# More expert groups ahead of layer 0's dense stage, gate multiplies on ScalarE, and split weights in the latent DeltaNet

## The chip, the cores and the metric

The kernel runs on one core of a Trainium2 chip. The core has TensorE (PE) for matmuls, VectorE (DVE), ScalarE (ACT) and GpSimd (POOL) for elementwise work, SyncE (SP), which issues most of the DMAs, and 16 DMA engines; each engine works its own instructions in order and waits for others by semaphores. The metric is the device time of one execution in microseconds (us). Three executions of the kernel before took 4279.19, 4285.04 and 4299.03 us; the median is 4285.04.

## The reference

The reference computes one block (a mixer of three branches and a convolutional feed-forward), and then a second block with two layers, each a mixer and a PEER layer, over 256 latent tokens and 256 context tokens of width 1024. The mixer of layer 0 is a gated DeltaNet, that of layer 1 attention. What the change touches is the DeltaNet and PEER:

```python
# PEER: 8 heads, 128 x 128 experts, 16 chosen per head
qry = (xb @ w_query).reshape(P, PEER_HEADS, 2, PEER_HALF)
s = jnp.einsum('phcd,hckd->phck', qry, sub_keys)
top_s, top_i = lax.top_k(s, PEER_TOPK)
...                       # 256 candidates of two halves, top 16 again
gate = jax.nn.softmax(best_s, axis=-1)
act = jax.nn.gelu(jnp.einsum('pd,phkd->phk', xb, u_tab[idx]))
coef = gate * act
return jnp.einsum('phk,phkd->pd', coef, v_tab[idx])
# DeltaNet
proj = h @ w_in           # 1024 -> 6208: q, k, v, z, gates
...                       # causal chunks of 64 tokens, 16 heads, both directions
return (rmsnorm_2(o, norm_g) * silu(z)).reshape(B, T, 2048) @ w_out
```

## The kernel before

The program runs, in order: conditioning vectors, the DeltaNet over the context tokens (51 to 580 us of the profiled execution), the first block (580 to 1550), the DeltaNet over the latent tokens (1550 to 2215), the latent PEER layer 0 (2215 to 3235), attention (to about 3440) and the latent PEER layer 1 with the final norm. The context tokens' PEER layer is worked differently from the latent one: its chosen experts are gathered from DRAM by index (POOL, L1908), multiplied and summed on DVE (dots L1931 `sg`, sums L1937 `spy`). This sparse work is a generator that other stages draw from (`bg`, with rates `bg_l`, `bg_dense` and the like), so its instructions stand between theirs on DVE and POOL.

A latent PEER layer (`peer_lat`) treats all experts densely, in 128 groups of 128. It has these stages:

- Routing (`route`): scores on PE (L1782), top-k on DVE. Since PE has little to do there, `ahead` gives it the u products of the first 20 groups, with plain f32 weights (L2018), into tiles `ge`. Behind the last top-k, indices `gi` and gates `gate` are transposed on PE (L1966) into `gT`.
- Building G (`build_G`): for each token a 128 x 128 matrix of gates, as a product of two one-hot matrices. For four tokens, DVE compares an iota with the second index (`gB`, L1979) and, token by token, with the first index and multiplies by the gate (`gA`, L1986); PE multiplies (L1989), ACT evicts (`Gs`, L1990), SP stores it in DRAM (`d_G`).
- Dense stage: for each group g, `dense_c` multiplies the activations `ge` with G and splits the result in two (`ch`, `cl`, L2030 to L2035); `dense_v` loads and splits the v weights (`vh` on ACT L221, `vl` mostly on POOL L222, every second one on DVE from group 108) and multiplies (L2054 to L2056, accumulators `acc`); `dense_u` makes the u product of group g + 20 with split weights (`uh` on ACT, `ul` on DVE; `mm3`, L226 to L228). From group 108 on there is none left.

A split writes an f32 number as a sum of two rounded fp32r numbers; three fp32r matmuls (`mm3`) then stand for one f32 matmul, which shows as two PE records in the trace.

The DeltaNet (`deltanet`) first makes gates and keys (`dn_gates`, `dn_k`, `dn_base`), then loops over 16 steps, eight key heads by two halves (`dn_heads`), in which `prep` of a later step, `chain` of the present one and the projections (`step`) of a later head are interleaved by generators; then comes the output projection (`out_res`, L391, L629). For the context tokens the weights are split (`wlo<-wraw,whi` on DVE); for the latent tokens `dn_32` has plain f32 weights, with the buffers of raw, high and low parts all used for raw weights (`wide = 3`). The loop looks two steps ahead, and of the farther `prep` makes four pieces (`dn_half`). `DN_BUFS` has the buffers of each tile.

The kernel is written in a framework that places waits and orders instructions on each engine by its own rules, so the order of instructions on an engine differs from the order of the code.

## Time and profile before

| | us |
|---|---|
| median of three executions | 4285.04 |
| profiled execution | 4293.87 |
| its span | 4292.0 |
| PE busy | 3590.3 (84%) |
| DVE busy | 2840.1 (66%) |
| POOL busy | 1953.9 (46%) |
| ACT busy | 1763.6 (41%) |
| mean granted TensorE clock | 0.909 of full speed |

The profile is of one execution. Busy time counts an engine's instructions, not its waits; PE's records overlap, since matmuls are pipelined, so the mean time of one is a latency and the pace of a run of them is read from its start times. A granted clock of 1 is 2.4 GHz, 0.5 is 1.2 GHz. "Idle before" is the time in which the engine waited ahead of an instruction, with the instruction that ended the wait.

### The profile page before, as it was taken

How to read it: one execution, taken by the hardware profiler on the slowest of the kernel's cores; microseconds unless marked ns; L12 is line 12 of the kernel's file. 1: busy time of each engine (PE TensorE's matmuls, PEld its weight loads, DVE VectorE, ACT ScalarE, POOL GpSimd, SP SyncE). 2: the span in 40 equal slices, each digit the busy share in tenths (PEclk: the TensorE clock that was granted, in tenths of full speed). 3: DMA queues.
4: the chain of work that ended last, by engine and by line, in shares of the span. 5: the costliest groups of instructions: out<-in, count | busy, mean ns of one | idle time of the engine just before them, and what ended most of it. 6: DMA issues, size and time to landing. Idle time of an engine off the chain costs nothing. (4 is left out here: it accounts for less than half of the span.)

```text
span 4292.0 us, 65372 instructions
## 1 busy us (share of the span) xinstructions
PE 3590.3 (84%) x23973; PEld 3148.1 (73%) x23973; DVE 2840.1 (66%) x5803; ACT 1763.6 (41%) x3352; POOL 1953.9 (46%) x1576
## 2 busy tenths in 40 slices
PE   6678879687777784787689679999987999899998
PEld 4667778576667763666668568988866889799987
DVE  2755456877788966756646978888896367644435
ACT  3445444236334432223211335555544313455555
POOL 1234412453466654547720149888873000344454
PEclk8789989789788996888799899999998999999999
DMA  8567553664577788888765679988973346666655
GB/s 284 182 178 227 136 161 116 239 227 151 192 278 248 263 316 246 271 260 274 237 218 194 222 236 327 344 319 324 331 270 117 107 152 187 224 214 207 218 173 186
DMA packets 423993, 971.83 MB, mean 226 GB/s; under 512 B 70322, under 2 KB 211834, under 8 KB 418938
## 3 DMA queue, kind: packets, MB, share of 16 engines
q1 hardware_dynamic: 349946, 699.20, 49.8%
q0 software_dynamic: 73728, 268.47, 17.8%
q8 instruction: 189, 3.10, 0.3%
q14 instruction: 130, 1.06, 0.1%
HBM read 898.66 MB, written 68.88 MB: 225 GB/s over the span
## 5 line engine op out<-in xcount | busy, mean ns | idle before, releaser
L222 POOL TENSOR_TENSOR vl<-vr,vh 128x512 fp32r<-128x512 f32 x460 | 651.3, 1434 | 757.3 <-ACT vh L221 751.9
L1908 POOL DMA_INDIRECT sg<-in_peer_u_dram,sidx x256 | 329.1, 1286 | 405.1 <-DVE sg L1931 205.0
L1937 DVE SCALAR_TENSOR_TENSOR spy<-sg,sact,spy 128x1024 f32<-128x1024 f32 x254 | 428.0, 1685 | 28.5 <-DMA sg<-in_peer_v_dram,sidx 27.2
L1931 DVE SCALAR_TENSOR_TENSOR sg<-sg,sph 128x1024 f32<-128x1024 f32 x256 | 376.3, 1481 | 98.0 <-DMA sg<-in_peer_u_dram,sidx 97.8
L228 PE MATMUL pact<-plhh,ul 128*128 128x256 f32 x1520 | 431.6, 284 | 0.0
L227 PE MATMUL pact<-plhl,uh 128*128 128x256 f32 x1520 | 431.4, 284 | 0.0
L226 PE MATMUL pact<-plhh,uh 128*128 128x256 f32 x1520 | 430.9, 284 | 0.1
L2055 PE MATMUL acc<-vl,ch 128*128 128x512 f32 x1024 | 407.4, 398 | 27.2 <-POOL vl L222 18.2
L1908 POOL DMA_INDIRECT sg<-in_peer_v_dram,sidx x256 | 318.0, 1242 | 244.1 <-DVE spy L1937 135.4
L2056 PE MATMUL acc<-vh,cl 128*128 128x512 f32 x1024 | 400.7, 391 | 0.0
L2054 PE MATMUL acc<-vh,ch 128*128 128x512 f32 x1024 | 353.0, 396 | 30.2 <-ACT vh L221 30.2
L221 ACT ACTIVATE whi<-wraw 128x1024 fp32r<-128x1024 f32 (+2 forms) x253 | 264.0, 1048 | 255.3 <-PE mm L227 60.0
L222 POOL TENSOR_TENSOR wlo<-wraw,whi 128x1024 fp32r<-128x1024 f32 (+1 forms) x94 | 234.1, 2501 | 295.4 <-PE mm L228 89.3
L221 ACT ACTIVATE vh<-vr 128x512 fp32r<-128x512 f32 x512 | 307.5, 624 | 115.9 <-PE acc L2056 93.6
L222 DVE TENSOR_TENSOR ul<-ur,uh 128x1024 fp32r<-128x1024 f32 x190 | 268.1, 1412 | 102.5 <-PE pact L228 95.3
L227 PEld LDWEIGHTS pact<-plhl,uh 128*128 128x128 f32 x1520 | 291.2, 192 | 10.1
L226 PEld LDWEIGHTS pact<-plhh,uh 128*128 128x128 f32 x1520 | 291.4, 192 | 9.6 <-ACT uh L221 0.2
L228 PEld LDWEIGHTS pact<-plhh,ul 128*128 128x128 f32 x1520 | 291.3, 192 | 4.5 <-issue 0.4
L222 DVE TENSOR_TENSOR wlo<-wraw,whi 128x1024 fp32r<-128x1024 f32 (+2 forms) x159 | 199.4, 1260 | 129.8 <-ACT whi L221 68.5
L221 ACT ACTIVATE uh<-ur 128x1024 fp32r<-128x1024 f32 x190 | 201.2, 1059 | 176.2 <-PE pact L227 170.9
L2055 PEld LDWEIGHTS acc<-vl,ch 128*128 128x128 f32 x1024 | 193.2, 189 | 75.9 <-POOL vl L222 29.9
L2031 DVE TENSOR_TENSOR co<-co,G 128x256 f32<-128x256 f32 x256 | 167.5, 655 | 122.1 <-ACT co L2030 98.6
(653 smaller groups left out, 9725.7 us busy)
## 6 DMA issues: line engine op xcount, KB each, us to landing
vr<-in_peer_v_dram SPq DMA_DIRECT2D x256, 512.0 KB
ur<-in_peer_u_T_dram SPq DMA_DIRECT2D x190, 512.0 KB
wraw<-in_ada_w_dram SPq DMA_DIRECT2D x96, 512.0 KB
wraw<-in_dn_w_in_dram SPq DMA_DIRECT2D x96, 512.0 KB
wraw<-in_peer_u_T_dram SPq DMA_DIRECT2D x66, 512.0 KB
wraw<-in_w_in_dram SPq DMA_DIRECT2D x64, 512.0 KB
d_G<-Gs SPq DMA_DIRECT2D x32, 1024.0 KB
G<-d_G SPq DMA_DIRECT2D x32, 1024.0 KB
```

Of the source, the lines that this page charges most:

```text
L221: nc.scalar.activation(hi, src, AF.Copy)
L222: (nc.gpsimd if pool else nc.vector).tensor_tensor(lo, src, hi.bitcast(F32), ALU.subtract)
L226: mm(out, lh, rh, start=start, stop=False)
L227: mm(out, lh, rl, start=False, stop=False)
L228: mm(out, ll, rh, start=False, stop=stop)
L1908: nc.gpsimd.indirect_dma_start(out=g, out_offset=None, in_=A[tab][0], in_offset=bass.IndirectOffsetOnAxis(ap=self.s_idx[:, t, j:j + 1], ax ...
L1931: nc.vector.scalar_tensor_tensor(g, g, 1.0, h, op0=ALU.mult, op1=ALU.mult, accum_out=act[:, j:j + 1])
L1937: nc.vector.scalar_tensor_tensor(y, g, act[:, j:j + 1], y, op0=ALU.mult, op1=ALU.add)
L2031: nc.vector.tensor_tensor(co, co, D["G"][:, :, g % 8], ALU.mult)
L2054: mm(acc[t][h], ch[:, tt], vh[h], start=first, stop=False)
L2055: mm(acc[t][h], ch[:, tt], vl[:, hh], start=False, stop=False)
L2056: mm(acc[t][h], cl[:, tt], vh[h], start=False, stop=last)
```

## The change

The change has four parts.

1. PEER layer 0: `ahead` makes 36 groups instead of 20 (`made`). Those from 20 on put their activations into a tile `gx` of two buffers and from there, by SP, into DRAM (`d_ge`, 128 KB a group); in the dense stage `dense_back` loads them in iterations 0 to 15, in the place of a u product. The dense stage keeps 92 u products of 108.
2. Building G, both layers: for four tokens, DVE compares the first index for three tokens in one instruction over 384 columns, ACT multiplies these three by the gates, one instruction each; the fourth token is done as before.
3. DeltaNet: the latent tokens use split weights like the context tokens. The loop looks one step ahead in whole pieces (`dn_ahead`), and the tiles `P`, `v`, `qT` and `kk` lose a buffer each, as does `rp` of the context tokens.
4. The rate of the sparse work in the latent DeltaNet goes from 4.5 to 3.3 (`bg_l`).

```diff
-    dn_half = 4
-    dn_32 = dict(c=False, l=True)
+    dn_ahead = dict(c=1, l=1)
+    dn_32 = dict(c=0, l=0)
...
-    DN_BUFS = {"c": dict(RB=3, P=3, rp=2, vn=2, kns=2, Se=1, S=3, o=1, v=3, z=3, qT=2, kk=2),
-               "l": dict(RB=3, P=3, rp=1, vn=1, kns=2, Se=1, S=3, o=1, v=3, z=3, qT=2, kk=2)}
+    DN_BUFS = {"c": dict(RB=3, P=2, rp=1, vn=2, kns=2, Se=1, S=3, o=1, v=2, z=3, qT=1, kk=1),
+               "l": dict(RB=3, P=2, rp=1, vn=1, kns=2, Se=1, S=3, o=1, v=2, z=3, qT=1, kk=1)}
...
-        late = {}
-        for i in range(-2, 16):
+        n = self.dn_ahead[which]
+        for i in range(-n, 16):
             gens = [chain(i)] if i >= 0 else []
-            if i + 1 in late:
-                gens.append(late.pop(i + 1))
-            new = prep(i + 2) if i + 2 < 16 else None
-            left, turn = self.dn_half if new else 0, 0
-            while gens or left:
+            if i + n < 16:
+                gens.append(prep(i + n))
+            while gens:
                 gens = [g for g in gens if next(g, self) is not self]
-                if left and (turn % 2 or not gens):
-                    next(new)
-                    left -= 1
-                turn += 1
                 self.tick()
                 if i >= 0:
-                    step(min(7, (i + 4) // 2))
-                    if i < 6:
+                    step(min(7, (i + n + 2) // 2))
+                    if i < 8 - n:
                         next(base, None)
...
-    backlog = (20, 46)
+    backlog, made = (20, 46), (36, 46)
...
-                if (q // 4) % self.g_mod < self.g_mul:
-                    nc.vector.tensor_tensor(a, io, i1T[:, tt:tt + 4].unsqueeze(2).to_broadcast([P, 4, P]), ALU.is_equal)
-                    nc.gpsimd.tensor_tensor(a, a, gT[:, tt:tt + 4].unsqueeze(2).to_broadcast([P, 4, P]), ALU.mult)
-                else:
-                    for i in range(4):
-                        t = tt + i
-                        nc.vector.tensor_scalar(a[:, i], self.iota, i1T[:, t:t + 1], gT[:, t:t + 1], op0=ALU.is_equal, op1=ALU.mult)
+                m = self.g_act
+                nc.vector.tensor_tensor(a[:, :m], io[:, :m], i1T[:, tt:tt + m].unsqueeze(2).to_broadcast([P, m, P]), ALU.is_equal)
+                for i in range(m):
+                    nc.scalar.activation(a[:, i], a[:, i], AF.Copy, scale=gT[:, tt + i:tt + i + 1])
+                for i in range(m, 4):
+                    t = tt + i
+                    nc.vector.tensor_scalar(a[:, i], self.iota, i1T[:, t:t + 1], gT[:, t:t + 1], op0=ALU.is_equal, op1=ALU.mult)
...
+        away = self.backlog[layer] <= g < self.made[layer]
+        ge = self.pge.tile([P, 256], F32, name="gx" if away else "ge", bufs=2 if away else self.backlog[layer] + 2)
         nc.scalar.activation(ge, pa, AF.Gelu)
-        D[g] = ge
+        if away:
+            nc.sync.dma_start(self.d_ge[g - self.backlog[layer]], ge)
+        else:
+            D[g] = ge
+
+    def dense_back(self, layer, g, D):
+
+        D[g] = self.pge.tile([P, 256], F32, name="ge", bufs=self.backlog[layer] + 2)
+        self.load(D[g], self.d_ge[g - self.backlog[layer]])
...
-                    if g + B + i < P:
+                    if M <= g + B + i < P:
                         self.dense_w(layer, g + B + i, D)
                 self.dense_v(layer, g, D, pv, acc)
-                if g + B < P:
+                if g + B < M:
+                    self.dense_back(layer, g + B, D)
+                elif g + B < P:
                     self.dense_u(layer, g + B, hT, D)
...
-        n = self.backlog[layer]
+        n = self.made[layer]
...
-    rate_c, rate_l, bg_m, bg_b1, bg_l, n_sg = 0.3, 0.3, 3.5, 3.5, 4.5, 4
+    rate_c, rate_l, bg_m, bg_b1, bg_l, n_sg = 0.3, 0.3, 3.5, 3.5, 3.3, 4
```

What it does to the order of instructions is shown at three places. The first is PE at the end of layer 0's routing, before, from its last score matmuls (`at`) to the transposes of `gi` and `gate`; `pact` are the u products ahead, `mps` small matmuls for conditioning vectors:

```order
L1782 MATMUL at<-skT,qry 128x128 x4
L2018 MATMUL pact<-plf,wraw 128x256 x32
L420 MATMUL mps<-wraw,cs_114 32x256 x4
L2018 MATMUL pact<-plf,wraw 128x256 x8
L420 MATMUL mps<-wraw,cs_114 32x256 x2
L2018 MATMUL pact<-plf,wraw 128x256 x8
L420 MATMUL mps<-wraw,cs_114 32x256 x2
L2018 MATMUL pact<-plf,wraw 128x256 x40
L1966 MATMUL tr<-ident,gi_19807 128x128 x2
L420 MATMUL mps<-wraw,cs_114 32x256 x8
L1966 MATMUL tr<-ident,gi_19808 128x128 x2
```

Now, at the same place (the line numbers of the changed file differ by a few):

```order
L1771 MATMUL at<-skT,qry 128x128 x4
L2007 MATMUL pact<-plf,wraw 128x256 x168
L420 MATMUL mps<-wraw,cs_114 32x256 x4
L2007 MATMUL pact<-plf,wraw 128x256 x5
L1955 MATMUL tr<-ident,gi_21120 128x128 x2
L2007 MATMUL pact<-plf,wraw 128x256 x3
L420 MATMUL mps<-wraw,cs_114 32x256
L2007 MATMUL pact<-plf,wraw 128x256 x7
L1955 MATMUL tr<-ident,gi_21121 128x128 x2
L2007 MATMUL pact<-plf,wraw 128x256
```

The matmuls of u products between the last score and the first transpose go from 88 to 173, and 19 more stand between the transposes.

The second place is DVE at the end of layer 0's dense stage, before; `vl` and `cl` are splits, `co` the coefficients, `spy` the sparse sums, `dtmp` and `xres` read the accumulators:

```order
L222 TENSOR_TENSOR vl<-vr,vh 128x512
L1937 SCALAR_TENSOR_TENSOR spy<-sg,sact,spy 128x1024
L2031 TENSOR_TENSOR co<-co,G 128x256
L2035 TENSOR_TENSOR cl<-co,ch 128x256
L222 TENSOR_TENSOR vl<-vr,vh 128x512
L2035 TENSOR_TENSOR cl<-co,ch 128x256
L2031 TENSOR_TENSOR co<-co,G 128x256
L222 TENSOR_TENSOR vl<-vr,vh 128x512
L1937 SCALAR_TENSOR_TENSOR spy<-sg,sact,spy 128x1024
```

Now:

```order
L2029 TENSOR_TENSOR co<-co,G 128x256
L2033 TENSOR_TENSOR cl<-co,ch 128x256
L222 TENSOR_TENSOR vl<-vr,vh 128x512
L2029 TENSOR_TENSOR co<-co,G 128x256
L2033 TENSOR_TENSOR cl<-co,ch 128x256
L2029 TENSOR_TENSOR co<-co,G 128x256
L222 TENSOR_TENSOR vl<-vr,vh 128x512
L2033 TENSOR_TENSOR cl<-co,ch 128x256
L222 TENSOR_TENSOR vl<-vr,vh 128x512 x2
```

The sparse sums have gone from the last groups: in the last 24 groups DVE has 23 sparse instructions instead of 32, in the last eight 2 instead of 12, and behind the last group none instead of four.

The third place is DVE in the latent output projection, before; `sg` are the sparse dots, `rtmp` is the first read of a finished projection:

```order
L864 TENSOR_TENSOR co<-co,hnr 128x512
L1931 SCALAR_TENSOR_TENSOR sg,sact<-sg,sph 128x1024 x21
L629 TENSOR_TENSOR rtmp<-orp,dgbc 128x512
L1931 SCALAR_TENSOR_TENSOR sg,sact<-sg,sph 128x1024
L630 TENSOR_TENSOR xres<-xres,rtmp 128x512
```

Now, the last rows ahead of the same read:

```order
L222 TENSOR_TENSOR dyTl<-tr,dyTh 128x512
L222 TENSOR_TENSOR wlo<-wraw,whi 128x1024
L1920 SCALAR_TENSOR_TENSOR sg,sact<-sg,sph 128x1024 x2
L222 TENSOR_TENSOR wlo<-wraw,whi 128x1024
L1920 SCALAR_TENSOR_TENSOR sg,sact<-sg,sph 128x1024
L222 TENSOR_TENSOR wlo<-wraw,whi 128x1024
L1920 SCALAR_TENSOR_TENSOR sg,sact<-sg,sph 128x1024
L629 TENSOR_TENSOR rtmp<-orp,dgbc 128x512
```

Weight splits (`wlo`) and splits of the input (`dyTl`) stand between the dots now; 12 of the weight splits are in this projection, 36 in the heads loop before it. In building G of layer 0, which is not shown, DVE has 16 sparse dots where it had 5, and 6 `ul` splits where it had 10.

## Rows read from the trace of the kernel before

**Rows 1.** Windows: stretch, us; busy (count) of PE, PEld, DVE, ACT, POOL; clock, DMA share, GB/s.

```profile
205.00:515.00 310.00, 249.07 (x2623) 219.37 (x2621) 162.24 (x354) 143.51 (x277) 116.04 (x150) 0.90 0.64 178
1720.00:2115.00 395.00, 302.21 (x2365) 256.01 (x2363) 266.14 (x480) 111.61 (x238) 255.12 (x254) 0.82 0.84 258
...
2393.00:2525.00 132.00, 99.35 (x769) 86.55 (x768) 121.80 (x348) 53.13 (x85) 1.14 (x1) 0.98 0.68 208
2525.00:2602.00 77.00, 65.42 (x345) 55.06 (x346) 59.48 (x73) 37.21 (x79) 69.25 (x48) 0.94 0.88 316
2602.00:3130.00 528.00, 522.17 (x3321) 471.48 (x3321) 441.61 (x423) 284.66 (x553) 456.16 (x309) 1.00 0.91 329
3130.00:3235.00 105.00, 77.29 (x324) 54.85 (x322) 99.86 (x99) 41.34 (x88) 66.39 (x50) 0.96 0.70 243
3550.00:3700.00 150.00, 135.89 (x922) 126.34 (x920) 117.26 (x326) 55.95 (x96) 0.00 (x0) 0.98 0.64 193
```

**Rows 2.** PE's timeline, end of routing: start, us, instruction, [idle before <-releaser].

```profile
2311.34 1.05 PE L1782 MATMUL at<-skT,qry 128*128 128x128 f32 x8
...
2335.12 17.53 PE L2018 MATMUL pact<-plf,wraw 128*128 128x256 f32 x80
2387.39 0.69 PE L1966 MATMUL tr<-ident,gi 128*128 128x128 f32 x2 [34.73 <-DVE gi L1959]
...
2392.36 0.69 PE L1966 MATMUL tr<-ident,gate 128*128 128x128 f32 x2
```

**Rows 3.** Lines in layer 0's building of G: busy us, mean ns, idle before.

```profile
L1986 DVE TENSOR_SCALAR gA<-iotaf,gT 128x128 f32<-128x128 f32 x256 | 70.4, 331 | 0.0
...
L1979 DVE TENSOR_TENSOR gB<-iotaf,gT 128x512 f32<-128x512 f32 x63 | 42.5, 674 | 0.0
L1990 ACT ACTIVATE Gs<-mm 128x512 f32<-128x512 f32 x64 | 38.1, 597 | 60.0 <-PE mm L1989 60.0
```

**Rows 4.** Line L1589, an activation with a per-partition operand: ns min/median/max.

```profile
L1589 ACT ACTIVATE cRB<-cRB,dG x64: 384/390/403, 1628.8 to 2092.3; 128x128 f32<-128x128 f32 x64
```

**Rows 5.** PE's timeline amid layer 0's dense stage.

```profile
2702.80 0.40 PE L2055 MATMUL acc<-vl,ch 128*128 128x512 f32 x1
...
2703.73 0.28 PE L226 MATMUL pact<-plhh,uh 128*128 128x256 f32 x1
...
2705.88 0.40 PE L2054 MATMUL acc<-vh,ch 128*128 128x512 f32 x1
```

**Rows 6.** Lines of POOL, 2602 to 3130.

```profile
L222 POOL TENSOR_TENSOR vl<-vr,vh 128x512 fp32r<-128x512 f32 x186 | 290.8, 1583 | 17.9 <-ACT vh L221 16.5
...
L1908 POOL DMA_INDIRECT sg<-in_peer_v_dram,sidx x104 | 141.3, 1359 | 46.8 <-DVE spy L1937 27.3 <-issue 9.6 <-DVE sg L1931 1.4
```

**Rows 7.** Lines of the dense stage's end, 3130 to 3235.

```profile
L1937 DVE SCALAR_TENSOR_TENSOR spy<-sg,sact,spy 128x1024 f32<-128x1024 f32 x28 | 52.5, 1877 | 0.1
...
L222 POOL TENSOR_TENSOR vl<-vr,vh 128x512 fp32r<-128x512 f32 x23 | 33.7, 1468 | 6.8 <-ACT vh L221 6.4
...
L222 DVE TENSOR_TENSOR vl<-vr,vh 128x512 fp32r<-128x512 f32 x20 | 26.5, 1324 | 2.8 <-ACT vh L221 2.8
...
L2031 DVE TENSOR_TENSOR co<-co,G 128x256 f32<-128x256 f32 x18 | 11.7, 649 | 1.8 <-ACT co L2030 1.8
L2035 DVE TENSOR_TENSOR cl<-co,ch 128x256 fp32r<-128x256 f32 x20 | 8.2, 411 | 0.0
```

**Rows 8.** Lines of DVE: latent output projection (first), ctx heads loop (second).

```profile
L1931 DVE SCALAR_TENSOR_TENSOR sg<-sg,sph 128x1024 f32<-128x1024 f32 x22 | 27.3, 1249 | 23.9 <-DMA sg<-in_peer_u_dram,sidx 23.9
...
L222 DVE TENSOR_TENSOR wlo<-wraw,whi 128x1024 fp32r<-128x1024 f32 x32 | 41.2, 1291 | 51.2 <-ACT whi L221 48.4 <-PE mm L227 2.8
```

**Rows 9.** Window of the latent heads loop, instructions of tile mm alone.

```profile
1720.00:2115.00 395.00, 144.33 (x569) 113.77 (x567) 36.65 (x80) 15.11 (x36) 0.82 0.84 258
```

**Rows 10.** PE's timeline, latent DeltaNet: ahead of heads loop, output projection.

```profile
1650.45 1.12 PE L1396 MATMUL tr<-ident,dkn 128*128 128x128 f32 x4 [19.22 <-DVE dkn L1392]
...
2184.11 26.76 PE L391 MATMUL orp<-wraw,dyf 128*128 128x256 f32 x112 [17.31 <-DVE rtmp L629]
```

More of the change, by code (lines that the diff above doesn't have):

```diff
@@ L1240, in deltanet @@
         G = pm.tile([P, 8, 2, 2, 16], F32, name="dG")
-        self.wide = 3 if self.dn_32[which] else 1
         self.wu = self.unit32 if self.dn_32[which] else self.unit
@@ L1275, in deltanet @@
             gb1 = self.gate_bc(out_mod, 2, 0 if which == "l" else 1, ph, "dgbc")
-            yT = ph.tile([P, 16, 256], F32, name="dyf") if self.dn_32[which] else self.hT_tiles(ph, 16, 256, "dyT")
+            yT = self.hT_tiles(ph, 16, 256, "dyT")
             for k0 in range(0, 16, 2):
@@ L1279, in deltanet @@
                 self.load(y, d_y[:, :, ds(k0 * P, 256)].rearrange("t p c -> p t c"))
-                self.transp_split(y, 2, yT[:, ds(k0, 2)] if self.dn_32[which] else (yT[0][:, ds(k0, 2)], yT[1][:, ds(k0, 2)]), 2)
+                self.transp_split(y, 2, (yT[0][:, ds(k0, 2)], yT[1][:, ds(k0, 2)]), 2)
             x = self.px.tile([P, 2, 1024], F32, name="xres", tag="x", bufs=1)
@@ L2018, in dense_u @@
                 nc.tensor.matmul(pa, u[:, k], hT[:, k], start=k == 0, stop=k == 7)
-        ge = self.pge.tile([P, 256], F32, name="ge", bufs=self.backlog[layer] + 2)
+        away = self.backlog[layer] <= g < self.made[layer]
+        ge = self.pge.tile([P, 256], F32, name="gx" if away else "ge", bufs=2 if away else self.backlog[layer] + 2)
         nc.scalar.activation(ge, pa, AF.Gelu)
-        D[g] = ge
+        if away:
[5 more added lines that the diff above has]
+        self.load(D[g], self.d_ge[g - self.backlog[layer]])
     def dense_c(self, g, D, pv):
@@ L2063, in peer_lat @@
         self.es_ps.close()
-        B = self.backlog[layer]
+        B, M = self.backlog[layer], self.made[layer]
+        if M > B:
+            self.d_ge = self.dram.tile([M - B, P, 256], F32, name="d_ge")
         with ExitStack() as es:
```

7 lines of the change are left out of this document (2 added, 5 removed).

## The prediction

> **What bounds the kernel now.** I read the page first. TensorE (PE) is busy 84% of a span of 4292.0 us and VectorE (DVE) 66%, as the table of times has them; that is an average over stages, so the second view is the table of windows, cut where the program changes stage [rows 1]. The reader should see four different limits there. In the long middle of layer 0's dense stage (2602 to 3130) PE is busy 522 of 528 us at full clock: TensorE-bound. In its last stretch (3130 to 3235) PE falls to 77 of 105 us and DVE is at 100: VectorE-bound, since expert groups without a u product are left. In building G of layer 0 (2393 to 2525) DVE is busy 122 of 132 us. In the heads loop of the latent DeltaNet (1720 to 2115) nothing is full: PE 302, DVE 266, POOL 255 of 395 us, with the DMA engines at 0.84, so it is bound by its chains of waits. The third view, PE's timeline at the end of the routing [rows 2], shows PE out of work: its last filler matmul ends at 2352.6 and the next one, a transpose of gi, waits 34.73 us for DVE, which works off the top-k.
>
> **Routing.** The change puts 16 more f32 expert groups (128 matmuls, two records each) into that hole. One record costs 17.53/80 = 0.219 us [rows 2]. In the new order 173 f32 matmuls stand between the last score and the gi transpose: 173 x 2 x 0.219 = 75.8 us from 2312.4, so to 2388.2, plus 4 small ones. DVE has gi ready at 2387.4: the hole is filled almost exactly and gi is no later than about 1 us. But 19 more f32 matmuls (8.3 us) now stand between gi and the gate transposes, with 4 small ones instead of 16; before, gate followed gi by 4.97 us [rows 2], most of it small matmuls. The first gA comes about 6 us later. Cost +6; if DVE is late, 0; if the 16 extra weight loads of 512 KB come late, up to +15.
>
> **Building G, layer 0.** Per four tokens before: one gB (42.5/63 = 0.675 us) and four gA (70.4/256 = 0.275 each), 1.775 us of DVE [rows 3]. After: gB, one comparison over 384 columns, one gA. The trace has no such comparison; by the two sizes it has (0.275 at 128, 0.675 at 512, though of different forms) it lies between 0.275 and 0.675; I take 0.54. That is 1.49 us, 0.285 less, times 64 = -18. The order now has 16 sparse dots inside this stage where 5 stood (and 2 behind it), 13 x 1.24 = +16 by the dot's row [rows 8], and 6 u splits instead of 10, -4 x 1.29 = -5. DVE's net: -7, with +6 from the late start: -1, which I take; a 0.40 us comparison makes it -10, a 0.675 one +8. ScalarE gets three multiplies per four tokens. The nearest row is an activation of the same 128x128 size with a per-partition operand, 390 ns [rows 4]. Beside Gs (0.597) that is at most 64 x (3 x 0.390 + 0.597) = 113 us, plus the stage's u splits and other work, about 12: 125, against a DVE of about 115. With instructions overlapping as in the window before, where 64 Gs took 38.1 us [rows 3], it is less; so ScalarE is close but second. The Trainium skill speaks against the move ("ScalarE: Activation LUTs", Rules for kernel authors: multiplies belong on VectorE, not ScalarE). By that rule the stage would be bound by ScalarE at 125 us and the case would come out at about +9 instead of -1; the same page (What ACT_TABLE_LOAD costs) has activations that follow each other overlap by about 93 ns, which would make the three cheaper than 0.390 each; no row shown here tests that.
>
> **Dense stage, layer 0.** 92 instead of 108 groups have a u product in it. One product is 24 records in a run at (2705.88 - 2703.73)/18 = 0.119 us, so 2.87 us; the v product is 12 at (2703.73 - 2702.80)/4 = 0.233, so 2.79 [rows 5]. Together 5.66 us; the trace has 3321 records at 36 per group, 92 groups, in 528 us: 5.74 each [rows 1].
> - Groups 0 to 16 took 77 us with POOL at 69 [rows 1]. After, most have no u product (6 are done by group 16, where 16 were), which frees PE but not POOL: two vl splits and 1.4 gathers, 2 x 1.58 + 1.4 x 1.36 = 5.1 us per group [rows 6], is more than 77/17 = 4.5 already. So nothing is gained; 16 reloads and stores of 128 KB come on top. I take +2 (-15 if DVE takes some splits, +8 for late reloads).
> - Groups 16 to 104 run 0.98 instead of 1 u product each: 88 x 0.06 = -5.
> - Groups 104 to 128: DVE-bound. Before: 24 x (0.65 + 0.41) for the coefficients, 20 vl x 1.32, 32 sparse adds x 1.88 [rows 7] and 5 u splits of 1.29: 25 + 27 + 60 + 6 = 118, near the 115 us from 3107 (2602 + 88 x 5.74) to 3222. After: no splits and 23 sparse adds: 95. PE's v products alone are 24 x 2.79 = 67. I take -20 of the -23. If POOL binds the groups at 5.1, nothing comes (24 x 5.1 = 122).
> - Behind the last product two sparse adds and the two sums stood ahead of xn on DVE; now nothing does: -4.
>
> **Layer 1.** Its building of G is PE-bound for the most part (136 of 150 us, DVE 117 [rows 1]); only its end can shrink: -3 (0 to -6). Peer in all: -1 + 2 - 5 - 20 - 4 - 3 = -31, between -55 and -5.
>
> **DeltaNet.** Latent projections go from f32 (2 x 0.219 = 0.438 per k-tile) to three fp32r products (3 x 0.119 = 0.358). In the heads loop that is 569/2 = 284 k-tiles [rows 9]: -23 us of PE at full clock. Against it DVE gets 36 weight splits in the loop, 12 in the output projection and the other 16 ahead of the loop, 1.29 us each by the ctx stage's row [rows 8]: +46, +15, +21. ScalarE gets as many, in a stage where it is 28% busy [rows 1]: nothing. What matters is how much of each is on the path. DVE is busy 67% of this loop and PE 77%: an instruction put into such a stream delays something about as often as the engine is busy, so 46 x 0.67 = +31 and -23 x 0.77 = -18: +13. Ahead of the loop the same reckoning gives some +7 for 16 splits and about 110 k-tiles, and a stall of 19.22 us there, in which PE waits for a key product that stands on POOL behind steps waiting for loads [rows 10], may shrink: +3. Bounds for the two: all of PE's gain, none of DVE's work and no stall, -45; all DVE work and a late reload at each of the seven head changes, since kk and qT have one buffer now, +75 (a reload is an estimate, 2 to 4 us: the stall of 19.22 over the five loads in it is 3.8).
> In the output projection PE waits 17.31 us for the first rtmp, which stands behind 21 dots on DVE [rows 10]; those are paced by their gathers (22 dots: 27.3 us busy, 23.9 idle [rows 8]). After, 18 dots stand ahead of rtmp with 6 weight splits and 8 y splits, about 13 us, which fit into the idle part. Behind it PE has 6.6 us less to do, and 6 dots and 6 splits stand between the first and the last rtmp: -4 (-15 to +15). The ctx stage keeps its arithmetic and loses buffers and half a step of lookahead: its splits waited for weights already. +4 (-5 to +15). I take DeltaNet at +16.
> The splits read two SBUF operands beside POOL's elementwise work. The trace shows POOL's vl at 1583 ns in the middle of the dense stage, with DVE adds running [rows 6], and 1468 in its end [rows 7]. The Trainium skill ("SBUF — State Buffer", section "SBUF: two separate sides") calls the port pair shared by the two engines an exclusive lock that blocks the loser for a whole instruction; by it the 36 splits would cost POOL up to 46 us in the loop too, which speaks for the slower side; no row here separates a lock from ordinary slowing.
>
> **Sum.** -31 + 16 = -15 us. The profiled execution took 4293.87 us (span 4292.0), 9 us above the median of 4285.04; it goes to about 4279, and the median to 4270.
>
> **Rivals.**
> 1. DeltaNet gains as well. Its loop is bound by PE's work and by stalls of the old half-step order; the new order spreads the projections more evenly. For: PE is the busiest engine there (77%), and the ctx loop, with split products and no sparse work, took 310 us for the same heads [rows 1]. Against: DVE waits are the longest ones in the loop. DeltaNet -35: 4285 - 31 - 35 = 4219.
> 2. The other side: the latent loop goes DVE-bound. Its 36 splits stand in order behind sparse dots and adds that wait for gathers, so weights come late to PE, the raw buffers (5 instead of 14) stay full and the loads on SP stop. Decides from the point where DeltaNet costs more than 55 us; priced by the whole of its DVE splits in loop and output projection, 62 us: 4285 - 31 + 62 = 4316.
> 3. The dense stage keeps its time: POOL at 5.1 us per group binds the groups that lose their u product, at the front and at the end. Peer then gives -1 + 2 - 4 - 3 = -6: 4285 - 6 + 16 = 4295. Against: at the end DVE takes 20 of the 48 vl.
>
> **Numbers.** Chances: the forecast 0.45 (own range 4248 to 4293), rival 1 0.21, rival 2 0.20, rival 3 0.14. ScalarE binding the building of G, to which I give one chance in ten within each case, moves the sum by 10 us and leaves it inside their ranges. The range reaches into rivals 1 and 2: 4213 to 4320. What a measurement here can tell from no change is 0.5%, 21.4 us: faster is below 4263.6, slower above 4306.5. Of the forecast some 0.17 lies below that line, with rival 1's 0.21 and 0.02 of rival 3: faster 0.40. Slower: 0.17 of rival 2 and 0.03 of rival 3: 0.20. Within: 0.40.
>
> **What would show it.** Right: PE without a hole before the gi transpose, gi at the same time, gate some 6 us later; building of G at 110 to 130 us with ScalarE at 80 to 110; 24 groups without u at the end at about 3.8 us each; the latent heads loop 395 to 425 us with PE idle on wlo. Wrong: the end of the dense stage with POOL as the releaser, the loop under 380 or above 450 us, or the ctx loop moved by over 15 us from 310.

## The result and the profile after

The changed kernel is slower: 4310.78 us median of 12 runs (4301.51 to 4317.77) against 4284.99 us (12 runs) of the kernel before, ratio 1.0062 (95% interval 1.0053 to 1.0072). The profiled execution took 4317.77 us with a span of 4315.7, which is 23.7 more than the span of before; the mean granted clock was 0.904.

The windows of the changed kernel, one row a stretch: us, then busy us (count) of PE, PEld, DVE, ACT, POOL, granted clock, DMA share, GB/s. They answer to [rows 1].

```profile
205.00:515.00 310.00, 251.60 (x2603) 221.58 (x2603) 161.00 (x353) 152.01 (x281) 113.33 (x151) 0.88 0.64 182
1720.00:2135.00 415.00, 287.32 (x2646) 258.22 (x2644) 315.05 (x528) 151.24 (x276) 274.68 (x259) 0.79 0.82 251
...
2400.00:2420.00 20.00, 20.00 (x150) 17.60 (x149) 11.94 (x28) 12.64 (x36) 2.08 (x2) 1.00 0.72 228
2420.00:2540.00 120.00, 85.39 (x603) 74.18 (x602) 100.59 (x213) 90.25 (x239) 17.73 (x15) 0.92 0.90 284
2542.00:2615.00 73.00, 56.17 (x214) 41.14 (x215) 59.12 (x65) 26.93 (x59) 60.78 (x46) 0.87 0.80 278
2615.00:2657.00 42.00, 38.75 (x224) 33.08 (x224) 39.24 (x43) 19.58 (x42) 32.43 (x24) 1.00 0.82 296
2657.00:3132.00 475.00, 459.43 (x2858) 408.13 (x2856) 434.85 (x347) 243.96 (x480) 395.90 (x266) 1.00 0.88 316
3132.00:3255.00 123.00, 95.84 (x404) 72.19 (x404) 99.48 (x99) 52.09 (x111) 79.33 (x56) 0.94 0.68 241
```

Two readings. In the first 20 us of building G (2400 to 2420) PE is full and DVE is busy for only 11.94 of them. Before, PE was just as full in the first 20 us, but DVE was too:

```profile
2393.00:2413.00 20.00, 19.94 (x196) 15.97 (x196) 19.88 (x47) 11.37 (x18) 1.14 (x1) 0.98 0.97 332
```

And in the long middle of the dense stage (2657 to 3132) PE is no longer full (459 of 475, against 522 of 528 before) while DVE has gone up to 435 of 475.

So that kernels can be compared, I cut each trace at the same events: the last score of layer 0's routing, the first gate transpose, the 64th `Gs`, the coefficient product `co` of groups 0, 24 and 104, the last product of the dense stage, and the first `Gs` of layer 1. Us between these events, from the start and end times in the traces:

| | before | after | e2_peer | e4_gact | e8_made28 | e10_route36 | e9_front0 | e11_made30 |
|---|---|---|---|---|---|---|---|---|
| score to gate | 80.0 | 87.6 | 87.9 | 80.2 | 80.8 | 104.7 | 86.1 | 84.0 |
| gate to 64th Gs | 124.2 | 127.8 | 127.7 | 111.7 | 112.1 | 105.5 | 134.9 | 105.5 |
| to co of group 0 | 10.0 | 12.2 | 12.3 | 10.2 | 10.4 | 10.3 | 10.3 | 10.4 |
| groups 0 to 24 | 111.7 | 117.5 | 113.2 | 111.7 | 119.1 | 115.0 | 81.2 | 95.5 |
| groups 24 to 104 | 458.0 | 475.5 | 475.5 | 459.4 | 468.0 | 478.0 | 461.7 | 464.8 |
| 104 to the last product | 128.4 | 121.4 | 115.1 | 126.4 | 122.5 | 122.8 | 129.5 | 129.1 |
| to layer 1's first Gs | 330.0 | 324.6 | 324.2 | 329.4 | 325.2 | 322.3 | 331.1 | 324.8 |

Between before and after these sum to +24.3 us, with the middle of the dense stage (+17.5), the gates (+7.6) and the front (+5.8) on one side and the end (-7.0 and -5.4) on the other; layer 1 from its first `Gs` on takes the same time within 0.2 us. The rest (+3.6 and +2.2) stands in building G and the step behind it.

Each column is one execution, and the profiled ones are not all near their medians: that of before is 9 us above it, that of after 7, that of e10_route36 12. Stretches that are the same code in two kernels differ between profiles: the latent heads loop took 333 to 337 us in the thirteen kernels that have the DeltaNet of before, building G 127.7 us in e2_peer and 134.9 in e9_front0, and groups 24 to 104 took 451 to 469 us in the kernels that leave this stage's code alone (before, e1_dn, e4_gact, e12_one_ahead). A difference of that size in one stretch is read only where several runs show it. Nor does this pair place the DeltaNet's part: the last score ends at 2312.4 us before and at 2311.7 after, and at 2296 to 2310 in the other twelve kernels with the old DeltaNet.

The routing and the first products of G, PE's timeline after (start, us, instruction), answering to [rows 2]:

```profile
2388.52 0.38 PE L1955 MATMUL tr<-ident,gi 128*128 128x128 f32 x2
...
2399.31 0.44 PE L1955 MATMUL tr<-ident,gate 128*128 128x128 f32 x2
2399.58 5.35 PE L2007 MATMUL pact<-plf,wraw 128*128 128x256 f32 x24
2404.76 1.95 PE L1978 MATMUL mm<-gB,gA 128*128 128x128 f32 x16
2406.55 4.48 PE L2007 MATMUL pact<-plf,wraw 128*128 128x256 f32 x20
```

The hole ahead of gi is filled and gi is 1.1 us later (1.8 counted from the last score); the gate transposes are 7 us later, as forecast. But behind them 24 and 20 records of u products stand ahead of G's products.

The lines of building G after (busy us, mean ns | idle before), answering to [rows 3, 4]:

```profile
L1972 ACT ACTIVATE gA<-gA,gT 128x128 f32<-128x128 f32 x192 | 62.7, 391 | 6.4 <-DVE gA L1970 5.0 <-DVE gT L1957 0.4
L1968 DVE TENSOR_TENSOR gB<-iotaf,gT 128x512 f32<-128x512 f32 x61 | 41.6, 682 | 0.0
...
L1970 DVE TENSOR_TENSOR gA<-iotaf,gT 128x384 f32<-128x384 f32 x62 | 34.1, 550 | 12.7 <-PE mm L1978 12.6
L1975 DVE TENSOR_SCALAR gA<-iotaf,gT 128x128 f32<-128x128 f32 x64 | 23.4, 365 | 0.0
L1920 DVE SCALAR_TENSOR_TENSOR sg<-sg,sph 128x1024 f32<-128x1024 f32 x18 | 21.8, 1216 | 0.0
```

The comparison over 384 columns costs 0.55 us (0.54 was taken), and the ScalarE multiplies 62.7/192 = 0.33 us each, though the record of one lasts 391 ns: they overlap. DVE waited 12.6 us for PE to give back `gA` buffers; that wait did not exist before, and most of it lies in the first 30 us, so the u products left over hold up G's products there.

The later part of the stage, from the 16th to the 64th `Gs`, has no u product before, and few after. Windows of it, of before, after and e4_gact (an experiment below, with the ScalarE multiplies alone):

```profile
2438.39:2516.59 78.20, 55.87 (x384) 48.07 (x384) 77.03 (x238) 28.66 (x49) 0.00 (x0) 1.00 0.57 162
2442.22:2527.11 84.89, 65.09 (x401) 57.45 (x399) 81.38 (x169) 72.38 (x193) 13.39 (x12) 0.94 0.87 264
2428.35:2493.29 64.94, 61.21 (x379) 52.06 (x377) 62.47 (x139) 64.51 (x189) 0.00 (x0) 1.00 0.69 196
```

DVE is the fullest engine before and after. In this part it has no sparse dot before and in e4_gact, and 13 after: at 1.22 us each these are 16 of the 20 us between after and e4_gact.

### The profile page after: what moved, and what is told of

It reads as the page before. It is cut to its first block, busy times and chain, and to the rows that moved or that the text cites. A ratio compares the mean times of both kernels' runs of the same rounds, so it can differ in the third digit from the quotient of the medians.

```text
span 4315.7 us, 66531 instructions
## 1 busy us (share of the span) xinstructions
PE 3594.7 (83%) x24365; PEld 3168.6 (73%) x24365; DVE 2935.2 (68%) x5606; ACT 1935.1 (45%) x3793; POOL 1978.7 (46%) x1576
## 5 line engine op out<-in xcount | busy, mean ns | idle before, releaser
L221 ACT ACTIVATE whi<-wraw 128x1024 fp32r<-128x1024 f32 (+2 forms) x318 | 332.5, 1049 | 337.1 <-DMA wraw<-in_dn_w_in_dram 82.5
L1926 DVE SCALAR_TENSOR_TENSOR spy<-sg,sact,spy 128x1024 f32<-128x1024 f32 x254 | 463.1, 1823 | 27.3 <-DMA sg<-in_peer_v_dram,sidx 26.0
L1897 POOL DMA_INDIRECT sg<-in_peer_v_dram,sidx x256 | 351.8, 1374 | 219.7 <-DVE spy L1926 126.8
L222 DVE TENSOR_TENSOR wlo<-wraw,whi 128x1024 fp32r<-128x1024 f32 (+2 forms) x224 | 295.0, 1320 | 160.5 <-ACT whi L221 94.0
L226 PE MATMUL pact<-plhh,uh 128*128 128x256 f32 x1392 | 394.7, 284 | 1.3 <-ACT uh L221 0.7
L228 PE MATMUL pact<-plhh,ul 128*128 128x256 f32 x1392 | 394.7, 284 | 0.0
L227 PE MATMUL pact<-plhl,uh 128*128 128x256 f32 x1392 | 394.6, 283 | 0.0
L2007 PE MATMUL pact<-plf,wraw 128*128 128x256 f32 x1312 | 292.6, 379 | 1.0 <-ACT gx L2010 0.9
L226 PEld LDWEIGHTS pact<-plhh,uh 128*128 128x128 f32 x1392 | 266.4, 191 | 14.3 <-ACT ge L2010 1.1
L227 PEld LDWEIGHTS pact<-plhl,uh 128*128 128x128 f32 x1392 | 266.4, 191 | 12.2
L2007 PEld LDWEIGHTS pact<-plf,wraw 128*128 128x128 f32 x1312 | 245.8, 190 | 34.5 <-ACT gx L2010 2.2
```

Of the source, the lines that this page charges most:

```text
L221: nc.scalar.activation(hi, src, AF.Copy)
L222: (nc.gpsimd if pool else nc.vector).tensor_tensor(lo, src, hi.bitcast(F32), ALU.subtract)
L226: mm(out, lh, rh, start=start, stop=False)
L227: mm(out, lh, rl, start=False, stop=False)
L228: mm(out, ll, rh, start=False, stop=stop)
L1897: nc.gpsimd.indirect_dma_start(out=g, out_offset=None, in_=A[tab][0], in_offset=bass.IndirectOffsetOnAxis(ap=self.s_idx[:, t, j:j + 1], ax ...
```

## The experiments

**The change in two halves.** e1_dn has the DeltaNet part alone, e2_peer the PEER part alone, e3_made and e4_gact the two halves of that.

```diff
 e1_dn: the DeltaNet lines of the change and bg_l 3.3
 e2_peer: all its other lines
 e3_made: +    backlog, made = (20, 46), (36, 46)   (with d_ge, dense_back)
 e4_gact: +    g_act = 3                            (with the lines of build_G)
```

> The kernel before with the DeltaNet part of the change alone (split weights for the latent tokens, one step of lookahead, fewer buffers, bg_l 3.3). Theory A (the loss is made in PEER layer 0; the DeltaNet part is neutral, since the latent heads loop gets some 25 us longer and the output projection some 21 us shorter, as the trace of the changed kernel has it): ratio to before 0.998 to 1.002. Theory B (the loss comes from the DeltaNet part, which leaves another distribution of the sparse work to the stages behind it): ratio 1.004 to 1.008.

> The kernel before with the PEER part alone (36 groups ahead and the ScalarE multiplies; DeltaNet and bg_l as before). Theory A: ratio 1.004 to 1.008, with the gate transposes about 7 us later, building G of layer 0 no shorter, the groups 16 to 104 of the dense stage at 5.8 to 5.9 us instead of 5.7. Theory B: ratio below 1.000, as the prediction had PEER alone at -31 us (0.993).

> The kernel before with 36 groups ahead alone (gates as before on DVE). Theory A in its first form (the 16 groups ahead cost: gates 7 us late behind f32 matmuls, 11 more sparse dots on DVE inside building G, DVE instructions lengthened in the dense stage): ratio 1.005 to 1.010, building G of layer 0 some 14 us longer than before (11 x 1.24). Theory A in its second form (the ScalarE multiplies cost, by a longer chain DVE, ScalarE, PE): ratio 0.995 to 1.001.

> The kernel before with the ScalarE multiplies alone. First form: building G of layer 0 shrinks from 121 us by 10 to 18 us, since DVE has 0.3 us less for four tokens and the number of dots stays at 5; that of layer 1 by 0 to 4; ratio 0.995 to 0.998. Second form: building G at 121 us or more in both layers, ratio 1.000 to 1.005.

Measured: e1_dn 1.0024 (1.0012 to 1.0037), e2_peer 1.0037 (1.0024 to 1.0051), e3_made 1.0075 (1.0057 to 1.0093), e4_gact 0.9984 (0.9971 to 0.9996). The halves add up to the whole: 10 + 16 = 26 us. Neither A nor B was right alone; by the ratios PEER has the larger share, though the two intervals overlap, and within it the 36 groups lose some 32 us while the ScalarE multiplies gain 7 by themselves and 16 beside the 36 groups. The windows of building G, from the first `Gs` to about the 64th, of e3_made and then e4_gact:

```profile
2392.40:2523.90 131.50, 101.00 (x720) 87.90 (x719) 127.36 (x356) 48.54 (x80) 17.71 (x16) 0.91 0.83 257
```

```profile
2386.70:2493.30 106.60, 102.51 (x724) 89.18 (x722) 100.24 (x210) 100.73 (x269) 0.00 (x0) 1.00 0.75 228
```

With the multiplies alone the stage takes 107 instead of 121 us and three engines are nearly full (PE 103, DVE 100, ACT 101), so the longer chain of engines is no loss. From the 16th `Gs` on ScalarE is the fullest of them, 64.51 of 64.94 us in the window above: four tokens take 1.35 us there, where DVE needed 1.63 before. ScalarE has become the limit of this part, and the part is still 13 us shorter. With 36 groups alone DVE is full at 127 of 131.

**How many groups fit into the hole.** e8_made28 and e10_route36 are the PEER part with other counts; e5_few_dots takes sparse steps away.

```diff
 e8_made28:   -    backlog, made = (20, 46), (36, 46)
              +    backlog, made = (20, 46), (28, 46)
 e10_route36: -    ... u_lag, u_route = ... (18, 8), (18, 30)
              +    ... u_lag, u_route = ... (12, 8), (36, 30)
 e5_few_dots: -    ... bg_dense, bg_ahead ... = ... 1.4, 1.0 ...
              +    ... bg_dense, bg_ahead ... = ... 1.4, 0.556 ...
```

> The PEER part alone with 28 instead of 36 groups ahead, 10 dots inside building G. If the 36 groups overfill PE's hole in the routing: gates follow gi by 5 us again instead of 11, PE idles some 20 us before gi, building G takes about 114 us, so 13 us less up to its end than e2_peer; the end of the dense stage keeps about half of its gain. If the slow middle of the dense stage comes with any groups ahead beyond 20, it stays at 514 us or more; if it comes with the crowding of 36, it is 500 to 508. Ratio to before 0.996 to 1.001.

> The PEER part alone with all 36 groups ahead issued within the routing (18 of them and the rest of the code's order inside building G before): no f32 matmul is left between the gate transposes and the end of building G, where 20 to 24 stood, and 4 dots instead of 16. Theory A (those f32 matmuls on PE hold up the first G products, and the dots DVE): building G 104 to 108 us instead of 121; gi 3 to 10 us later, since 192 f32 matmuls stand ahead of it, and gate 10 us behind gi as in e2_peer. Ratio to before 0.999 to 1.002. Rival (the longer chain of engines keeps building G at 118 or more): ratio 1.003 to 1.005.

> The PEER part alone with 20 instead of 36 sparse steps drawn by the groups ahead (bg_ahead 0.556): 9 dots instead of 16 inside building G of layer 0. Theory A (the dots drawn along with the groups are what lengthens building G): the stage goes from 121 to about 112 us (7 x 1.24), the gates stay 6 us late; some sparse work more falls into the dense stage and its end, +0 to +15. Rival (the chain DVE, ScalarE, PE sets the stage): 119 us or more. Ratio to before 0.999 to 1.005.

Measured: e8_made28 0.9992 (0.9981 to 1.0003), e10_route36 1.0017 (1.0004 to 1.0030), e5_few_dots 1.0049 (1.0035 to 1.0062). Windows of building G again, of e8_made28 and e10_route36:

```profile
2385.70:2493.00 107.30, 94.61 (x628) 82.62 (x626) 100.59 (x216) 96.21 (x260) 9.17 (x8) 0.94 0.81 249
```

```profile
2420.50:2520.10 99.60, 90.05 (x624) 76.84 (x622) 91.95 (x199) 94.67 (x260) 0.00 (x0) 1.00 0.78 239
```

With 28 groups none of the u products made ahead is left behind the gates, and building G takes 107 us even with 10 dots in it (114 was expected). From the gate to the 16th `Gs` it takes 38.5 us where e2_peer takes 44.3 with as many dots (5): that is the price of the u products at the start. From there to the 64th it takes 73.5 with 5 dots and e2_peer 83.4 with 13: that is the price of the dots. Groups 16 to 104 take 514 us with 28 groups too, so the slow middle does not need the full 36. e10 moves all u products ahead of the gates, building G falls to 100 us, gi comes 14 us later than in e2_peer (3 to 10 was expected), and the time comes back in the row above it: score to gate 104.7 instead of 87.9. PE's hole in the routing holds 34.73 us [rows 2], ten groups of 3.5 us; 16 groups are 56 us, and the 21 us too many are paid on one side of the gates or on the other. e5_few_dots missed its mark: the framework put 40 instead of 24 matmuls of u products behind the gates when there were fewer dots, so gi came 9 us earlier than in e2_peer, the stage stayed at 122 us from first to 64th `Gs`, and this run by itself does not separate the two.

**The dense stage without sparse work.**

```diff
-    bg_r, bg_dense, bg_ahead ... = 0.0, 1.4, 1.0 ...
+    bg_r, bg_dense, bg_ahead ... = 0.0, 0.0, 1.0 ...
```

> The PEER part alone (as e2_peer), with no sparse work drawn in the dense stage of layer 0 while u products are left (bg_dense 0); the sparse work left over runs in one piece behind the stage, so only the dense stage's groups 16 to 104 are read, not the total. Theory C (the sparse instructions on DVE, crowded beside POOL's splits, slow the stage; in the changed kernel they fall into a worse order): 496 to 503 us for these 88 groups, 5.64 to 5.72 each, no longer than e7_before_no_sparse by more than 3. Theory D (the new order of u products keeps PE waiting by itself): 508 us or more, at least 8 longer than e7_before_no_sparse.

> The kernel before with no sparse work drawn in the dense stage of layer 0, read as e6_no_sparse. Both theories: 496 to 503 us for groups 16 to 104, against 494 to 507 with the sparse work in it.

Windows of e6_no_sparse (groups 0 to 16, 16 to 24, 24 to 104), then of e7_before_no_sparse (0 to 16, 24 to 104); the windows of groups 0 to 16, here and below, leave out their first 2.5 to 3 us:

```profile
2537.00:2578.50 41.50, 39.44 (x164) 31.77 (x164) 13.92 (x27) 24.84 (x57) 35.42 (x29) 0.92 0.77 255
2578.50:2602.60 24.10, 24.10 (x123) 20.37 (x122) 10.25 (x18) 15.94 (x34) 21.44 (x17) 1.00 0.71 244
2602.60:3051.20 448.60, 448.60 (x2874) 409.35 (x2873) 184.06 (x241) 249.48 (x480) 205.64 (x160) 1.00 0.63 212
```

```profile
2517.00:2567.80 50.80, 50.80 (x276) 44.66 (x277) 20.14 (x32) 32.05 (x67) 36.05 (x28) 0.95 0.71 241
...
2612.80:3062.50 449.70, 449.70 (x2883) 410.44 (x2882) 183.76 (x241) 249.61 (x480) 206.10 (x161) 1.00 0.64 211
```

Without sparse work both kernels run the middle at 5.6 us a group with PE full, and groups 0 to 24 take 98.4 us before and 68.5 after: the change does save 30 us there. With it the same groups take 111.7 and 113.2 (e2_peer). My numbers for groups 16 to 104 were 496 to 503 for both; e7 had 494.7, e6 472.7, since it has no u products up to about group 22, which I had not counted. Theory D falls; of theory C it is shown that the sparse work slows the stage, and not that its order does. What the sparse work does to the instructions is in the lines of groups 24 to 104, of the changed kernel and of e6_no_sparse:

```profile
L222 POOL TENSOR_TENSOR vl<-vr,vh 128x512 fp32r<-128x512 f32 x160 | 248.3, 1572 | 8.8 <-ACT vh L221 7.5
L1926 DVE SCALAR_TENSOR_TENSOR spy<-sg,sact,spy 128x1024 f32<-128x1024 f32 x106 | 222.9, 2103 | 0.5 <-DMA sg<-in_peer_v_dram,sidx 0.2
...
L222 DVE TENSOR_TENSOR ul<-ur,uh 128x1024 fp32r<-128x1024 f32 x80 | 146.6, 1833 | 9.2 <-PE pact L228 6.5 <-ACT co L2028 1.4 <-ACT uh L221 1.0
```

```profile
L222 POOL TENSOR_TENSOR vl<-vr,vh 128x512 fp32r<-128x512 f32 x160 | 206.1, 1309 | 243.3 <-ACT vh L221 243.3
...
L222 DVE TENSOR_TENSOR ul<-ur,uh 128x1024 fp32r<-128x1024 f32 x80 | 98.3, 1229 | 81.0 <-PE pact L228 78.9 <-DMA ur<-in_peer_u_T_dram 2.0
```

The sums do not only take their own time: the u splits beside them go from 1.23 to 1.83 us and POOL's splits from 1.31 to 1.57. In the changed kernel's groups 8 to 24, where PE has no u product:

```profile
L1920 DVE SCALAR_TENSOR_TENSOR sg<-sg,sph 128x1024 f32<-128x1024 f32 x21 | 54.2, 2582 | 0.0
L222 POOL TENSOR_TENSOR vl<-vr,vh 128x512 fp32r<-128x512 f32 x32 | 43.9, 1394 | 4.0 <-ACT vh L221 3.7
```

A dot that took 1216 ns in building G, with POOL making no splits, takes 2582 on average here: 1366 more, about one `vl`. The start and end times tell the two cases apart within one stage. Of these 21 dots the five with no `vl` beside them take 1.27 us at most, the other 16 on average 3.0. In groups 24 to 104 of the changed kernel the 21 sums and 31 u splits with no `vl` beside them take 1.30 us at most; the 86 sums and 49 u splits with one take 2.3 and 2.2 on average, up to 4.7. Busy DMA engines are not the reason: the dots of 1216 ns stood in a window with a DMA share of 0.90. The longer records are what an engine that waits out a whole instruction of the other would show, as the Trainium skill has it ("SBUF — State Buffer", section "SBUF: two separate sides"). In groups 16 to 24 DVE is the full engine (39 of 42 us in the window 2615 to 2657); PE's freed time is not used.

**Sparse work out of the front.** The PEER part with

```diff
-                self.bg(self.bg_dense if g + B < P else self.bg_tail)
+                self.bg(0.0 if g + B < M and layer == 0 else self.bg_dense if g + B < P else 0.7)
```

and `bg_dense` 1.65.

> The PEER part alone (as e2_peer), with no sparse work drawn in the 16 dense iterations that reload stored activations and 1.65 instead of 1.4 sparse steps in the others. Theory C (the groups without a u product give nothing back because sparse dots, at 2.6 us each beside POOL's splits, take the place of PE's work): groups 0 to 24 of layer 0's dense stage, 112 us in e2_peer, fall to 66 to 75, near the 66 of e6_no_sparse; the end of the stage gets 19 sparse instructions back and some 12 to 16 us longer. Rival (the front is bound by POOL's splits and the reloads, not by the sparse work): 100 us or more. For groups 24 to 104, 474 us in e2_peer: 458 to 466 if their slowness came from the order in which u splits, sums and coefficient splits stand on DVE, which is the more regular one of the kernel before here; 470 or more if the mere presence of the sums costs it. Ratio to before 0.993 to 1.001.

Measured 0.9975 (0.9963 to 0.9986). Groups 0 to 16, 16 to 24 and 24 to 104:

```profile
2534.50:2576.30 41.80, 40.23 (x165) 32.45 (x166) 13.99 (x28) 25.15 (x57) 35.93 (x29) 0.91 0.75 255
2576.30:2613.20 36.90, 35.20 (x186) 29.66 (x185) 29.14 (x29) 18.88 (x40) 33.03 (x25) 1.00 0.81 293
2613.20:3074.90 461.70, 448.06 (x2833) 402.22 (x2832) 441.59 (x365) 234.88 (x475) 392.86 (x266) 1.00 0.91 324
```

The front falls by 32 us (113.2 to 81.2; 66 to 75 was expected, but the sparse work resumes by group 16), the middle comes to 461.7, within the range given for the order as its cause, and the end gets 14 us back. What held the front at 113 us was the sparse work: without any it takes 68.5 (e6_no_sparse).

**What makes the middle slow.** The work of a group is the same in all kernels there, but its time is 451 to 478 us for 80 groups with the sparse work, even 468.9 in e12_one_ahead, which has PEER's code of before. The mix of the sparse work is not what sets it: in these groups the kernel before has 93 sums and 13 dots (458 us), the changed one 107 sums and no dots (475), but e5_few_dots has 93 sums and 14 dots and takes 477. Two runs move the place in the code where the sparse work is drawn, and with it the place of the sums on DVE.

```diff
 e13_before_draw_early: the call of self.bg stands behind dense_c, on the kernel before
 e14_peer_draw_first:   it stands first in the loop's body, on e2_peer
```

> The kernel before with the same sparse work drawn earlier in the code of each dense iteration (behind the coefficients instead of at its end), which moves sparse sums on DVE: of the groups 24 to 104, 29 instead of 13 have a sum directly behind the coefficient product, ahead of the coefficient split and the u split. In the runs so far the time of these 80 groups rises with that number (before 13: 458 us; 19: 459; 24 and 25: 462 and 465; 30 and 37: 469 and 468; 52: 475). If the order is the cause: 464 to 470 us. If it only went along with another cause (more groups ahead, another phase of the transfers), since nothing else is changed: 455 to 461.

> The PEER part alone (as e2_peer) with the sparse work drawn at the start of each dense iteration's code: 35 instead of 52 groups of 24 to 104 have a sum directly behind the coefficient product, 19 instead of 28 have the u split behind the coefficient split. If the order is the cause: 465 to 471 us for these 80 groups instead of 475. If not: 473 to 478.

Measured: e13 460.7 us (ratio of the whole 0.9988, 0.9973 to 1.0002), e14 471.9 (1.0008, 0.9994 to 1.0021). The first falls within the "not the cause" range, the second between its two ranges. In the trace e13 has 26 sums directly behind the coefficient product, twice as many as before, at 2.7 us more: that place is not what sets the time. The whole of e14 is some 12 us under e2_peer by the ratios, of which this stretch gives 3.6. Afterwards, another feature of the order goes with it better: the number of these 80 groups that have the u split behind the coefficient split is 0 to 2 in the kernels with 451 to 465 us, 9 to 20 in those with 468 to 472 and 28 or 29 in those with 475 to 478. That was found in the data and not tested by a run of its own; it stays open. What is shown is that PE waits more for POOL's splits. Waits of PE between 2610 and 3090, of before and of after (us in total, times, longest), and the window of groups 24 to 104 before, which answers to 2657 to 3132 after:

```profile
PE acc L2055 <- POOL vl L222: 4.7, 7, 1.2
```

```profile
PE acc L2053 <- POOL vl L222: 14.8, 31, 1.4
```

```profile
2638.20:3096.30 458.10, 452.60 (x2876) 408.64 (x2876) 383.71 (x361) 247.29 (x483) 393.56 (x267) 1.00 0.91 329
```

PE's idle time grows by 10 us (5.5 of 458 before, 15.6 of 475 after). The other 7 us are in its busy time, with no more matmuls; what lengthens them is open.

**The DeltaNet's parts.** e12_one_ahead has the new loop and buffers with plain f32 weights.

```diff
 e12_one_ahead: the loop lines and DN_BUFS of the change, and
-    dn_32 = dict(c=False, l=True)
+    dn_32 = dict(c=0, l=1)
```

> The kernel before with the new DeltaNet loop alone: one step of lookahead in whole pieces and the smaller buffers, but plain f32 weights for the latent tokens as before (bg_l 4.5). Theory A (the latent heads loop of the changed kernel is 22 to 25 us longer because of the 36 weight splits on DVE, and the context loop some 8 us longer because of the shorter lookahead): latent stretch from the first to the last pvn 330 to 345 us (337 before, 360 in e1_dn), context stretch 298 to 306, output projection at 95 to 98 as before; ratio 1.000 to 1.003. Rival (the shorter lookahead and the single kk and qT buffers make the latent loop longer too): latent stretch 352 or more, ratio 1.004 to 1.009.

Measured 1.0024 (1.0012 to 1.0036). From the first to the last `pvn` of the latent loop, e12_one_ahead and then e1_dn:

```profile
1772.80:2107.40 334.60, 250.86 (x2097) 212.87 (x2098) 230.11 (x394) 104.18 (x221) 221.54 (x232) 0.84 0.88 254
```

```profile
1774.00:2133.50 359.50, 247.16 (x2354) 222.44 (x2354) 280.31 (x465) 138.34 (x255) 248.38 (x239) 0.81 0.85 256
```

The loop takes 337.4 us before: the smaller buffers and the shorter lookahead cost the latent loop nothing, the split weights 22 to 25 us. The output projection gives back as much: 97.9 us from the last `pvn` to the last read before, 77.2 in e1_dn, 92.8 in e12_one_ahead. The context loop is 12 us longer from its first to its last `pvn` (291.7, 303.9, 303.8 in before, e1_dn and e12_one_ahead; 299.8 in the changed kernel), but begins 4 to 8 us earlier. Of e12's 10 us most are in the dense stage (468.9 against 458.0 for groups 24 to 104), whose code it leaves alone, while its last score ends at 2300.3 us like that of kernels with the old DeltaNet; e1_dn takes 451.2 us for the same groups. A change upstream is enough to move that stage by as much as the effects that were to be measured.

**A version that beats both.** The DeltaNet of before, the ScalarE multiplies, 30 groups ahead, all drawn within the routing (`u_lag` (8, 8), `u_route` (30, 30)), no sparse work in the reloading iterations, `bg_dense` 1.55.

```diff
 e11_made30: g_act = 3, d_ge, dense_back and the call of self.bg as in e9_front0, and
-    backlog = (20, 46)
+    backlog, made = (20, 46), (30, 46)
-    ... bg_dense, bg_ahead, u_lag, u_route = ... 1.4, 1.0, (18, 8), (18, 30)
+    ... bg_dense, bg_ahead, u_lag, u_route = ... 1.55, 1.0, (8, 8), (30, 30)
```

> A version meant to beat both: the DeltaNet of the kernel before, the ScalarE multiplies, 30 groups ahead, all issued in the routing (168 f32 matmuls between the last score and gi, none behind), no sparse work in the ten reloading iterations, 1.55 steps in the others. If the causes found so far hold: gates no later than before, building G 104 to 108 us, groups 0 to 16 of the dense stage 45 to 58 us instead of 64.5, groups 16 to 104 490 to 505, the end as before or some us longer. Ratio to before 0.990 to 0.996. If the middle of the stage stays slow as with 28 and 36 groups (514): 0.994 to 0.999.

Measured 4262.84 us, 0.9937 (0.9922 to 0.9953): 27 us under the kernel before, 53 under the changed one in ratios. Its windows of building G and of groups 0 to 16:

```profile
2395.10:2495.30 100.20, 92.79 (x624) 80.08 (x622) 94.31 (x203) 94.65 (x260) 0.00 (x0) 0.97 0.76 227
2508.20:2555.40 47.20, 46.18 (x217) 38.46 (x218) 20.97 (x32) 26.41 (x60) 40.77 (x32) 0.95 0.74 255
```

Building G at 100 us is under the 104 to 108 expected and the front at 47 is as expected; gi is 4 us later, against the expectation, and groups 16 to 104 missed the expectation (510.6 us from the first `co` to the last, not 490 to 505): the middle keeps over a third of its loss.

## Why the prediction was wrong

It forecast -15 us and got +26. By its own steps:

- Routing: right. gi +1.1 us and gate +7 were forecast as about +1 and +6. What it missed stands behind the gate: of the 128 matmuls added it placed 85 ahead of gi and 19 between gi and gate, and gave the other 24, 10.5 us by its own price, no place and no cost.
- Building G: DVE's work fell as reckoned (121.8 to 112.5 us busy in the stage's window; -7 was forecast, of which the comparison was right to 0.01 us), and the 16 dots cost what they were put at. The step that failed is "DVE sets the stage": DVE now waits 12.6 us for PE, most of it behind the u products left over, so its shorter work did not make the stage shorter. The stage with the gates was put at -1 and came to +11. ScalarE bound nothing in the changed kernel (72 of 85 us in the later part, DVE 81). In e4_gact it did bind that part, and the stage was 14 us shorter all the same: the Trainium skill's rule against multiplies there ("ScalarE: Activation LUTs", Rules for kernel authors) did not decide this case.
- Front of the dense stage: the sum put +2 for groups 0 to 16 and was right that nothing would be gained, but not in the reason. Its floor, POOL at 5.1 us a group, was above the 4.5 that it read for the kernel before (4.2 when cut at the coefficients), so it could not be a floor, and it counted sparse gathers. Without sparse work these 16 groups take 41.5 us with POOL at 35 (e6_no_sparse). Sparse work fills the time that the u products leave: DVE's dots last 2.58 us each, in place of the 1.25 of [rows 8]. DVE (59) and POOL (61 of 73 us) are about equally busy there, so which of them binds is not separated.
- Middle: this is the term that failed most. It took the 88 groups as PE-bound at 5.74 us, -5 in all; groups 24 to 104 alone got 17.5 us longer. Its own rows had DVE at 442 and POOL at 456 of 528 us beside a full PE [rows 1], and both runs without sparse work take 5.6 us a group, before and changed; the prediction read only the busiest engine and gave the sparse work beside it no cost. Why the sparse work costs 8 us there before (458 against 450) and 27 after (475 against 449) stays open.
- End: -20 forecast, -7 in the changed kernel and -13 in e2_peer. DVE's work fell as reckoned (118 to 95 was forecast, 117.4 to 98.1 measured), but "DVE-bound" failed: from group 104 to the last product DVE had been idle for 11 us before and is idle for 23 after. PE's waits there for DVE's splits fall from 8.5 to 4.8 us, those for POOL's rise from 5.1 to 12.4, and those for `vh` from 3.8 to 8.7. That is the sign of being wrong that the prediction gave, POOL as the releaser; but POOL itself waits 25 us there for `vh`, and ScalarE 12 us for the loads that `vh` is made from. The step behind the last product, -4, was right (-5.4). Layer 1, -3, gave nothing.
- DeltaNet: +16 forecast, +10 (5 to 16) measured. That the sum came near is luck, since its parts were off and cancelled: the latent loop +22 to 25 instead of +13, the output projection -21 instead of -4, outside its own -15 to +15. The +4 for the context tokens agrees (their last `pvn` ends 4 us later).

The windows from group 104 to the last product, before and after, on which the account of the end rests:

```profile
3096.30:3224.60 128.30, 110.67 (x536) 84.94 (x534) 117.38 (x109) 57.28 (x119) 94.07 (x70) 0.99 0.78 276
3132.20:3253.60 121.40, 95.81 (x404) 72.19 (x404) 98.08 (x96) 51.89 (x111) 79.13 (x56) 0.94 0.69 244
```

PEER was put at -31 and came to +16 (10 to 22). Rival 3, in which the dense stage keeps its time, was nearest in mechanism, but named POOL and had no term for a stage that gets slower; rival 2's 4316 was near the time, but its place was wrong: the DeltaNet cost 10 us, not 62.

## What to carry to other kernels

Filler work for a waiting engine is worth only as much as the hole holds: count it in us against the wait, and look at what stands behind the instruction that ended the wait, since what does not fit is paid there. Where background work is drawn per iteration, an iteration that gets lighter on one engine still carries the same background: move the draws with the time, not with the count. And where two engines beside the bound one are nearly full too (84 and 86% here), a change upstream alone moved the stage by several per cent (451 to 469 us with the same code), so a gain of a few us there can't be forecast from busy times.
